# Gate and up products of the feed-forward layers in seven block products instead of eight

## Chip, core and metric

The kernel runs on one core of one Trainium2 chip. The metric is the device time of one execution in microseconds (us). The engines are TensorE (PE, with its weight loads as PEld), VectorE (DVE), ScalarE (ACT), GpSimd (POOL) and SyncE (SP, which here issues most of the loads).

## What is computed

One inference step of a small decoder trunk, all in float32, for 512 prompt tokens and 8 sample tokens (520 columns). There are two layers; each has a feed-forward block before and after its mixer, so four feed-forward layers run:

```
def _swiglu(h, wg, wu, wd):
    return (jax.nn.silu(h @ wg) * (h @ wu)) @ wd

for i in range(DEPTH):                      # DEPTH = 2
    x = x + 0.5 * _swiglu(_rmsnorm(x, norm_ffn1[i]), ffn1_wg[i], ffn1_wu[i], ffn1_wd[i])
    # mixer: chunked gMLP (i = 0) or S5 state-space scan (i = 1)
    x = x + out
    x = x + _cross_attn(_rmsnorm(x, norm_x[i]), mem_k[i], mem_v[i], x_wq[i], x_wo[i])
    x = x + 0.5 * _swiglu(_rmsnorm(x, norm_ffn2[i]), ffn2_wg[i], ffn2_wu[i], ffn2_wd[i])
```

The model width is 1024 (8 k-tiles of 128), the hidden width is 2816 (22 tiles of 128).

## The kernel before

Activations are kept transposed: `X` holds 8 tiles of 128 features x 520 tokens. Each product runs in three matmuls: every operand is split into a high part (rounded to the fast float32 matmul format) and a low remainder, and high x high, high x low and low x high are added up in PSUM. `wsplit` (L110, L113) makes the two parts of 128 columns of weights: ACT writes `wh`, then DVE, or POOL for every fourth, subtracts to get `wl`. `split` (L139, L140) does the same for activations. `lin` issues the matmuls; all go through `mm`, so line L74 stands for nearly all of them. A matmul covers 260 tokens, half of the 520; an accumulator `ps` holds both halves, and there are four of them.

A feed-forward layer (`ffn`) takes x times the norm's gain as eight tiles `xs`; the scale per token, `rs`, is applied later. It then walks over 11 blocks of 256 columns. `gu(j)` loads 256 columns of gate and 256 of up (SP queue, three buffers `wr`), splits them (four buffers each of `wh` and `wl`), and for each 128 of them runs 48 matmuls for gate and 48 for up. DVE multiplies both by `rs` (L345, L347), ACT takes silu (L346), DVE multiplies (L348), and `split` writes a tile of `hid`. After every six tiles of `hid` (`FFN_GROUPS`) `down` multiplies them by the down weights and DVE adds the results to `X` (L361). One more block is always done ahead of a `down`. In the last layer of all, `last` takes the final group and `finish` interleaves the output.

`fill()` is called after each block and each `down` and traces a step of side work: memory keys and values and the gMLP's matrices during the first layer, and the S5 mixer's tables (`s5_prep`, mostly POOL, with DVE, ACT and PE pieces) during the second and third. The last layer has none. Temporary tiles `t` come from 12 buffers, large tiles (`xs`, `hid`, the tables) from 22 slots.

The order of instructions on each engine is fixed before the run by a scheduler that takes what is ready by its own cost figures, in priority of the program's order; at run time each engine follows that order and waits by semaphore.

Of the kernel before, what the change touches and what calls it, by code (L numbers as in the profile page):

```python
# [9 lines left out]
F32 = mybir.dt.float32  # L10
# [22 lines left out]
SLOTS = 22  # L33
WB = 4
FFN_GROUPS = ((0, 6), (6, 12), (12, 18), (18, 22))
BUFS = {"t": 12, "rs": 2, "rt": 4, "st": 10, "sti": 4, "mv": 4, "sc": 2, "cj": 2, "s5": 12, "s5i": 1,
# [3 lines left out]
class Prog:  # L40
# [15 lines left out]
    # ---------------------------------------------------------------- helpers  # L56
# [16 lines left out]
    def mm(self, out, lhsT, rhs, start, stop):  # L73
        self.nc.tensor.matmul(out, lhsT=lhsT, rhs=rhs, start=start, stop=stop)  # L74
# [5 lines left out]
    def in_order(self, *engines):  # L80
        """The engines issue what is traced here in the order of the program."""
# [21 lines left out]
    def wsplit(self, raw, m, eng=None):  # L103
        """128 columns of weights as two parts."""
# [11 lines left out]
    def wload(self, src, nk, cols):  # L116
        """A block of weights [(nk 128), cols], split into two parts per 128 columns."""
        raw = self.wraw(nk, cols)
        self.wget(raw, src, 0, cols)
        return [self.wsplit(raw, m) for m in range(cols // 128)]  # L120

    def lin(self, ps, w, xs, k0=0, k1=None, hs=(0, 1)):
        """ps[:, :, :HN] = w^T @ xs; only the k-tiles k0 to k1 and the halves hs of the tokens."""
# [93 lines left out]
    def rsqrt(self, out, var, scale):  # L217
        """out = (var * scale + eps) ** -0.5 for a few columns: a first guess and Newton steps."""
# [16 lines left out]
    def rs_tok(self, sq):  # L235
        """rsqrt(mean_d x[t]^2 + eps) per token, tokens on partitions: four chunks and the last 128 tokens."""
# [8 lines left out]
    def rs_diag(self, sq):  # L245
        """The same on the diagonals of squares, for rs_row."""
# [8 lines left out]
    def rs_row(self, dg):  # L255
        """The scales along the free dimension, the same in every partition."""
# [7 lines left out]
    def scaled(self, key, xs, n0=0, n1=NT):  # L264
        """x * gain in two parts per k-tile."""
# [6 lines left out]
    def norm(self, key):  # L272
        """x * gain in two parts per k-tile; the scale per token comes later."""
# [4 lines left out]
    # -------------------------------------------------------------------- ffn  # L278
    def ffn(self, l, pre, fill=lambda: None, start=False, finish=None):
# [12 lines left out]
        def begin():  # L292
            """The first columns, the first half of the tokens before the second has come."""
# [59 lines left out]

        def down(a, b):
# [10 lines left out]
        def last(a, b):  # L365
            """The last columns, one half of the tokens after the other, each followed by its part of finish."""
# [27 lines left out]
        for g0, g1 in FFN_GROUPS:  # L394
            while done < min(DFF // 256, g1 // 2 + 1):
                gu(done)
# [6 lines left out]
    # ----------------------------------------------------------- memory k, v  # L403
    def mem_kv(self, l, kvd):
        """Steps that put the memory's keys (transposed) and values into DRAM, kvd."""
# [68 lines left out]
    # -------------------------------------------------------- cross-attention  # L474
    def attn(self, l, kvd):
# [28 lines left out]
        # sample queries as rows, spread over all partitions one batch entry at a time  # L504
# [75 lines left out]
        # one column of 32 per batch entry, so that every (b, h) adds up in its own row  # L580
# [39 lines left out]
        def part(k0, k1):  # L620
            """Heads of the first 256 columns of the output, for the first half of the tokens."""
# [55 lines left out]
    # ---------------------------------------------------------- chunked gMLP  # L677
    def gmlp_prep(self, mixw):
        """Steps that make the causal mixing weights, transposed; their row sums; the bias per row."""
# [22 lines left out]
    def gmlp(self, mixw):  # L702
# [6 lines left out]
        # v: gelu, then tokens on the partitions; [token, (j, chunk, column)] per pair of column tiles  # L709
# [71 lines left out]
        # the sample rows, one token per chunk: mixed = w_s[0, 0] * v + b_s[0]  # L781
# [73 lines left out]
    # -------------------------------------------------------------------- S5  # L855
    def dexp(self, x, sh, em1=None):
        """exp(x), and exp(x) - 1 when asked for."""
# [21 lines left out]
    def s5_prep(self):  # L879
        """Steps that make the matrices and tables of the scan and put them in DRAM."""  # L880
# [34 lines left out]
        # theta in turns: wh (few bits) + wl  # L915
# [71 lines left out]
        # C and B-bar with the state on the partitions  # L987
# [3 lines left out]
        for c, n in enumerate("re im".split()):  # L991
            nc.gpsimd.dma_start(cr[c], ins["b_c_" + n][0].rearrange("(t g) c p -> (g c) t p", t=8))
            nc.gpsimd.dma_start(bn[:, c], ins["b_b_" + n][0].rearrange("(q g) p c -> (g p) q c", g=2))
# [130 lines left out]
    def s5(self, fill=lambda: None):  # L1124
# [11 lines left out]
        def lay(i):  # L1136
            """[8 sample | 128 blocks | 8 sample] columns per place in the block."""
# [10 lines left out]
        def spread(u4):  # L1148
            """Places in the block onto the partitions, per pair of groups."""
# [27 lines left out]
        def scan(i, sps):  # L1177
            """The states of the four pairs of groups of channel tile i."""
# [91 lines left out]
        def states():  # L1270
            """New states of the samples and last states of the prompt."""
# [29 lines left out]
    # ------------------------------------------------------------------ final  # L1301
    def final(self):
        """What follows the columns q of the last product for the tokens of half h."""
# [137 lines left out]
```

## Time and profile before

| | us |
|---|---|
| median of three runs | 2496.0 |
| lowest run | 2494.11 |
| highest run (stands far from the others) | 8334.05 |
| span of the profiled execution | 2493.1 |

The median lies 2.9 us above the profiled span and the lowest run 1.0 us; no time of its own is recorded for the profiled execution beside its span. PE has 20575 matmuls and as many weight loads. Busy times overlap across engines. A granted clock of 1.00 is the full TensorE clock.

### The profile page before, as it was taken

To read this page: it belongs to the slowest core of one execution; us is meant where nothing else is said; L and a number is where in the kernel's file an instruction comes from. 1 tells how busy PE (TensorE), PEld (TensorE's weight loads), DVE (VectorE), ACT (ScalarE), POOL (GpSimd) and SP (SyncE) were. 2 spreads that over 40 slices of the span, in tenths; PEclk is the share of its full clock that TensorE was granted. 3 is DMA by queue.
4 is the path that set the end of the run, shared out by engine and by line. 5 is a ranking of instruction groups with operands and counts; after the bars stand their busy time and mean duration, and the time that the engine had idled before them with its cause. 6 is when DMAs were issued, how large, how long until landed. Compare 5 with 4: busy or idle time off the path is not lost.

```text
span 2493.1 us, 47609 instructions
## 1 busy us (share of the span) xinstructions
PE 2419.0 (97%) x20575; PEld 2364.9 (95%) x20575; DVE 1342.0 (54%) x2304; ACT 803.6 (32%) x1239; POOL 556.4 (22%) x532
## 2 busy tenths in 40 slices
PE   8999999999999999999999999999779999999998
PEld 7999999999999799999999999999769969999998
DVE  6534343648556557455565645536973655434344
ACT  4323232432224342232342422424322324222223
POOL 2111011102111012262523515103452101101111
PEclk8999999999999999999999999999889999999999
DMA  5243432321225623334233324327523562232321
GB/s 171 94 131 114 136 102 85 119 85 55 85 90 198 226 96 90 102 100 138 98 111 110 131 95 132 122 69 247 192 87 107 169 237 85 80 107 83 96 77 52
DMA packets 247376, 293.40 MB, mean 118 GB/s; under 512 B 7358, under 2 KB 226230, under 8 KB 247166
## 3 DMA queue, kind: packets, MB, share of 16 engines
q1 hardware_dynamic: 234055, 254.88, 31.5%
q10 hardware_dynamic: 12567, 34.38, 3.9%
q8 instruction: 162, 2.65, 0.4%
q0 software_dynamic: 544, 1.10, 0.3%
q14 instruction: 48, 0.39, 0.0%
HBM read 264.77 MB, written 25.56 MB: 116 GB/s over the span
## 4 chain that ended last, share of the span: by engine, by line
PE 88%; DVE 6%; issue 2%; ACT 2%; POOL 1%; DMA 1%; DVEq 0%; ACTq 0%; POOLq 0%
PE ps L74 86%; PE ps L77 2%; DVE ld L1194 1%; DVE v L773 1%; DVE xs L269 1%; DVE sq L213 1%; DVE wl L113 0%; DVE t L533 0%; POOL ld L1190 0%; DMA vc<-in_cache_mem_v 0%; DVE hid L140 0%; ACT e L553 0%; ACT wh L110 0%; DMA ld<-s5tt 0%; DVE bi L1093 0%
## 5 line engine op out<-in xcount | busy, mean ns | idle before, releaser
L74 PE MATMUL ps<-xs,wh 128*128 128x260 f32 x7168 | 1164.1, 284 | 3.4 <-ACT xs L268 2.4
L74 PEld LDWEIGHTS ps<-xs,wh 128*128 128x128 f32 x7168 | 990.0, 189 | 6.8 <-ACT xs L268 2.8
L110 ACT ACTIVATE wh<-wr 128x1024 fp32r<-128x1024 f32 (+2 forms) x440 | 420.3, 958 | 1161.1 <-PE ps L74 1051.4
L74 PE MATMUL ps<-xs,wl 128*128 128x260 f32 x3584 | 725.9, 283 | 0.0
L113 POOL TENSOR_TENSOR wl<-wr,wh 128x1024 fp32r<-128x1024 f32 (+2 forms) x119 | 271.4, 2281 | 1608.0 <-ACT wh L110 1580.3
L74 PEld LDWEIGHTS ps<-xs,wl 128*128 128x128 f32 x3584 | 554.4, 189 | 0.0
L74 PE MATMUL ps<-hid,wh 128*128 128x260 f32 (+2 forms) x2816 | 457.0, 283 | 2.7 <-ACT hid L139 1.8
L113 DVE TENSOR_TENSOR wl<-wr,wh 128x1024 fp32r<-128x1024 f32 (+2 forms) x321 | 365.9, 1140 | 98.5 <-ACT wh L110 97.0
L74 PEld LDWEIGHTS ps<-hid,wh 128*128 128x128 f32 x2816 | 388.5, 188 | 4.6 <-ACT hid L139 2.4
L74 PE MATMUL ps<-hid,wl 128*128 128x260 f32 (+2 forms) x1408 | 288.0, 282 | 0.0
L74 PEld LDWEIGHTS ps<-hid,wl 128*128 128x128 f32 x1408 | 218.9, 188 | 0.0
L347 DVE TENSOR_TENSOR t<-ps,rs 128x520 f32<-128x520 f32 x88 | 61.4, 698 | 254.5 <-PE ps L74 254.5
L361 DVE SCALAR_TENSOR_TENSOR X<-ps,X 128x520 f32<-128x520 f32 x120 | 83.7, 698 | 211.6 <-PE ps L74 211.1
L345 DVE TENSOR_TENSOR t<-ps,rs 128x520 f32<-128x520 f32 x88 | 61.4, 697 | 182.5 <-PE ps L74 151.6
L140 DVE TENSOR_TENSOR hid<-t,hid 128x520 fp32r<-128x520 f32 x88 | 95.5, 1086 | 34.3 <-ACT hid L139 34.3
L139 ACT ACTIVATE hid<-t 128x520 fp32r<-128x520 f32 x88 | 56.3, 639 | 127.5 <-DVE t L348 127.4
L74 PE MATMUL ps<-o,wh 128*128 128x260 f32 x512 | 92.5, 290 | 1.2 <-DVE o L140 0.7
L74 PE MATMUL ps<-ms,wh 128*128 128x256 f32 x512 | 92.0, 282 | 0.8 <-DVE ld L1187 0.5
L74 PE MATMUL ps<-z,wh 128*128 128x260 f32 x512 | 84.6, 286 | 1.1 <-DVE z L140 0.5
L348 DVE TENSOR_TENSOR t<-t,t 128x520 f32<-128x520 f32 x88 | 78.9, 896 | 6.8 <-ACT wh L110 0.5
L74 PE MATMUL ps<-um,wh 128*128 128x260 f32 x512 | 82.5, 283 | 0.0
L74 PEld LDWEIGHTS ps<-o,wh 128*128 128x128 f32 x512 | 74.6, 188 | 7.4 <-issue 2.9
(316 smaller groups left out, 2406.3 us busy)
## 6 DMA issues: line engine op xcount, KB each, us to landing
wr<-in_ffn_wg SPq DMA_DIRECT2D x43, 1024.0 KB, 5.3
wr<-in_ffn_wu SPq DMA_DIRECT2D x43, 1024.0 KB, 5.2
wr<-in_ffn_wd SPq DMA_DIRECT2D x48, 768.0 KB, 4.8
wr<-in_a_w_in SPq DMA_DIRECT2D x16, 1024.0 KB, 5.8
kc<-in_cache_mem_k SPq DMA_DIRECT2D x32, 512.0 KB, 7.7
vc<-in_cache_mem_v SPq DMA_DIRECT2D x32, 512.0 KB, 5.8
wr<-in_x_wk SPq DMA_DIRECT2D x8, 1024.0 KB, 5.2
wr<-in_x_wv SPq DMA_DIRECT2D x8, 1024.0 KB, 5.2
```

What stands on the lines that cost most here:

```text
L74: self.nc.tensor.matmul(out, lhsT=lhsT, rhs=rhs, start=start, stop=stop)
L77: self.nc.tensor.transpose(out, in_, self.ident[base : base + k, base : base + k])
L110: nc.scalar.activation(hi, r, AF.Copy)
L113: eng.tensor_sub(lo, r, hi.bitcast(F32))
L139: nc.scalar.activation(sl[:, 0, n0:n1], src, AF.Copy)
L140: nc.vector.tensor_sub(sl[:, 1, n0:n1], src, sl.bitcast(F32)[:, 0, n0:n1])
L213: (nc.gpsimd if k == 7 and early or k < 4 and not early else nc.vector).tensor_add(sums[-1], sums[-1], t)
L269: self.nc.vector.scalar_tensor_tensor(s[:, 1, n0:n1], x, g, s.bitcast(F32)[:, 0, n0:n1], op0=ALU.mult, op1=ALU.subtract)
L345: nc.vector.tensor_mul(self.v2(t), pg[:, :, :HN], rs)
L347: nc.vector.tensor_mul(self.v2(w), pu[:, :, :HN], rs)
L348: nc.vector.tensor_mul(w, w, t)
L361: nc.vector.scalar_tensor_tensor(xv, p[:, :, :HN], 0.5, xv, op0=ALU.mult, op1=ALU.add)
```

## The change

All blocks of gate and up but the first of each layer go through `gu7` instead of `gu`. Weights and tokens are cut into 2 x 2 blocks: the 256 columns of a block into two halves of 128, the 1024 features into two halves of 512, the tokens into two halves of 260. The eight block products become seven, each of 24 matmuls for gate and up together; their operands are sums and differences of blocks (`seven_x` for the tokens, once per layer; `seven` for the weights, per block), and the results are sums of products, partly added in PSUM (an accumulator is written on after DVE has read it), partly by DVE. All low parts of these weights are DVE's. The down products take groups of four hidden tiles instead of six (the last layer of all ends as before), there are two more slots, two fewer temporary tiles, and one S5 transfer is cut into parts so that a smaller scratch suffices. The diff, without lines that only drop comments:

```diff
-SLOTS = 22
+SLOTS = 24
-FFN_GROUPS = ((0, 6), (6, 12), (12, 18), (18, 22))
-BUFS = {"t": 12, ...
+FFN_GROUPS = ((0, 4), (4, 8), (8, 12), (12, 16), (16, 20), (20, 22))
+END_GROUPS = ((0, 4), (4, 8), (8, 12), (12, 18), (18, 22))
+BUFS = {"t": 10, ...
+    def seven_x(self, key, xs):
+        xb = [[self.slot([128, 4, HN], F32, "xb") for _ in range(2)] for _ in range(2)]
+        for k in range(KT):
+            for h in range(2):
+                nc.scalar.activation(xb[k // 4][h][:, k % 4], self.X[:, k, h * HN : (h + 1) * HN], AF.Copy,
+                                     scale=self.gcol(key, k))
+        (b11, b12), (b21, b22) = xb
+        V.tensor_sub(b11, b12, b11)
+        V.tensor_sub(b12, b22, b12)
+        V.tensor_sub(b22, b22, b11)
+        V.tensor_sub(b21, b21, b22)
+        T = []
+        for b in (b11, b22, b12):
+            hi, lo = (self.slot([128, 4, HN], F32R, "xt") for _ in range(2))
+            nc.scalar.activation(hi, b, AF.Copy)
+            V.tensor_sub(lo, b, hi.bitcast(F32))
+            T.append([(hi[:, k], lo[:, k]) for k in range(4)])
...
+        def last():
+            for k in range(4):
+                self.split(xs[k], b21[:, k], HN, NT)
+        return {"B11": B[0], "B21": B[2], "B22": B[3], "T1": T[0], "T2": T[1], "T3": T[2], "T4": B[1]}, last
+    def seven(self, r1, r2, ops, ps):
+        sh = list(r1.shape[:3]) + [128]
+        A11, A21, A12, A22 = r1[..., :128], r1[..., 128:], r2[..., :128], r2[..., 128:]
+        n, nk = sh[1:3]
+        def parts(src):
+            hi = self.wp.tile(sh, F32R, name=self.nm("wh"), tag="wh", bufs=WB)
+            lo = self.wp.tile(sh, F32R, name=self.nm("wl"), tag="wl", bufs=WB)
+            nc.scalar.activation(hi, src, AF.Copy)
+            V.tensor_sub(lo, src, hi.bitcast(F32))
+            return hi, lo
+        def product(p, w, b, first):
+            hi, lo = w
+            for x in range(n):
+                for k in range(nk):
+                    bh, bl = ops[b][k]
+                    for i, (m, r) in enumerate(((hi, bh), (hi, bl), (lo, bh))):
+                        self.mm(p[:, x, :HN], m[:, x, k], r, first and k == 0 and i == 0, k == nk - 1 and i == 2,
+                                skip_group_check=not first)
+        S1, S2 = (self.wp.tile(sh, F32, name=self.nm("S"), tag="S", bufs=2) for _ in range(2))
+        w11 = parts(A11)
+        G.tensor_add(S1, A21, A22)
+        G.tensor_sub(S2, S1, A11)
+        a, b, c = (ps() for _ in range(3))
+        va, vb, vc = (p[:, :, :HN] for p in (a, b, c))
+        e1, e2, e3 = (self.tmp([128, 2, HN]) for _ in range(3))
+        product(a, w11, "B11", True)
+        nc.scalar.copy(e1, va)
+        product(b, parts(S2), "T2", True)
+        V.tensor_add(e2, vb, e1)
+        product(a, parts(A12), "B21", False)
+        yield "11", va
+        V.tensor_sub(A21, A11, A21)
+        V.tensor_sub(A12, A12, S2)
+        product(b, parts(A21), "T3", False)
+        V.tensor_add(e3, vb, e1)
+        product(c, parts(S1), "T1", True)
+        V.tensor_add(e3, vc, e3)
+        yield "22", e3
+        product(b, parts(A22), "T4", False)
+        V.tensor_add(e1, vb, e1)
+        yield "21", e1
+        product(c, parts(A12), "B22", False)
+        V.tensor_add(e2, vc, e2)
+        yield "12", e2
+        def gu7(j):
+            if ops is None:
+                ops, late = self.seven_x(key, xs)
+                late()
...
+            for i in range(2):
+                r.append(self.wp.tile([128, 2, 4, 256], F32, name=self.nm("wr"), tag="wr", bufs=3))
+                for x, w in enumerate((wg, wu)):
+                    nc.sync.dma_start(r[i][:, x], w[i * 512 : (i + 1) * 512, cs].rearrange("(k p) m -> p k m", p=128))
+            tw = [self.tmp() for _ in range(2)]
+            for name, v in self.seven(*r, ops, self.ps):
+                i, h = int(name[0]) - 1, int(name[1]) - 1
+                d = self.tmp([128, 2, HN]) if name == "11" else v
+                nc.vector.tensor_mul(d, v, rs[:, h : h + 1].to_broadcast([128, 2, HN]))
+                nc.scalar.activation(d[:, 0], d[:, 0], AF.Silu)
+                nc.vector.tensor_mul(tw[i][:, h * HN : (h + 1) * HN], d[:, 1], d[:, 0])
+                if name in ("21", "12"):
+                    hid[2 * j + i] = self.slot(name="hid")
+                    self.split(hid[2 * j + i], tw[i])
+            fill()
-        for g0, g1 in FFN_GROUPS:
+        for g0, g1 in END_GROUPS if finish else FFN_GROUPS:
-                gu(done)
+                (gu7 if done else gu)(done)
-            nc.gpsimd.dma_start(bn[:, c], ins["b_b_" + n][0].rearrange("(q g) p c -> (g p) q c", g=2))
+            for q in range(0, NPAIR, 16):
+                nc.gpsimd.dma_start(bn[:, c, q : q + 16], ...
-    nc = bacc.Bacc("TRN2", target_bir_lowering=False, num_devices=1)
+    nc = bacc.Bacc("TRN2", target_bir_lowering=False, num_devices=1, dynamic_dma_scratch_size=4096)
```

## Rows read from the trace of the kernel before

**Rows 1.** The page, parts 1 and 4: busy shares; the chain that ended last.

```profile
...
PE 2419.0 (97%) x20575; PEld 2364.9 (95%) x20575; DVE 1342.0 (54%) x2304; ACT 803.6 (32%) x1239; POOL 556.4 (22%) x532
...
PE 88%; DVE 6%; issue 2%; ACT 2%; POOL 1%; DMA 1%; DVEq 0%; ACTq 0%; POOLq 0%
PE ps L74 86%; PE ps L77 2%; DVE ld L1194 1%; DVE v L773 1%; DVE xs L269 1%; DVE sq L213 1%; DVE wl L113 0%; DVE t L533 0%; POOL ld L1190 0%; DMA vc<-in_cache_mem_v 0%; DVE hid L140 0%; ACT e L553 0%; ACT wh L110 0%; DMA ld<-s5tt 0%; DVE bi L1093 0%
...
```

**Rows 2.** Windows: layers, first block, two blocks, a down product, a burst.

```profile
core 0: us, PE busy (x) PEld busy (x) DVE busy (x) ACT busy (x) POOL busy (x), PEclk, DMA share, GB/s
...
32.00:440.00 408.00, 407.25 (x3367) 405.62 (x3368) 174.07 (x220) 122.60 (x161) 50.50 (x22) 0.99 0.35 112
910.00:1297.00 387.00, 383.28 (x3223) 381.02 (x3222) 217.32 (x375) 122.16 (x186) 130.47 (x160) 1.00 0.32 101
1297.00:1690.00 393.00, 388.13 (x3281) 384.78 (x3280) 215.54 (x332) 130.89 (x203) 125.02 (x154) 1.00 0.35 115
2094.00:2470.00 376.00, 376.00 (x3136) 375.56 (x3135) 164.36 (x204) 103.57 (x132) 44.27 (x23) 1.00 0.26 82
2094.00:2117.00 23.00, 23.00 (x192) 22.88 (x191) 14.24 (x29) 9.09 (x11) 2.42 (x1) 1.00 0.29 92
2131.00:2177.00 46.00, 46.00 (x387) 46.00 (x386) 20.76 (x23) 13.14 (x17) 5.61 (x2) 1.00 0.24 75
2192.00:2227.00 35.00, 35.00 (x294) 35.00 (x293) 12.65 (x15) 7.85 (x9) 4.24 (x2) 1.00 0.37 121
...
1065.00:1090.00 25.00, 25.00 (x212) 25.00 (x211) 12.79 (x12) 6.09 (x9) 19.67 (x37) 1.00 0.13 37
```

**Rows 3.** The chain in order of time: start us, us, what.

```profile
...
480.01 5.75 PE ps L74 x48
...
2139.99 328.32 PE ps L74 x2738
...
2476.68 2.85 PE ps L74 x24
...
```

**Rows 4.** Groups by shape: busy us, mean ns of one, idle before, releaser.

```profile
...
L110 ACT ACTIVATE wh<-wr 128x1024 fp32r<-128x1024 f32 x288 | 304.5, 1059 | 835.5 <-PE ps L74 735.0 <-issue 75.3 <-DVE t L1114 21.6
...
L361 DVE SCALAR_TENSOR_TENSOR X<-ps,X 128x520 f32<-128x520 f32 x120 | 83.7, 698 | 211.6 <-PE ps L74 211.1
...
L345 DVE TENSOR_TENSOR t<-ps,rs 128x520 f32<-128x520 f32 x88 | 61.4, 697 | 182.5 <-PE ps L74 151.6 <-POOL M L1041 30.5
...
L139 ACT ACTIVATE hid<-t 128x520 fp32r<-128x520 f32 x88 | 56.3, 639 | 127.5 <-DVE t L348 127.4
...
L268 ACT ACTIVATE xs<-X,gains 128x260 fp32r<-128x260 f32 x16 | 6.7, 500 | 0.0
...
```

**Rows 5.** DVE in order of time, last layer: start us, us, operation.

```profile
...
2155.34 1.22 DVE L113 TENSOR_TENSOR wl<-wr,wh 128x1024 fp32r<-128x1024 f32 x1
2156.48 0.69 DVE L140 TENSOR_TENSOR hid<-t,hid 128x520 fp32r<-128x520 f32 x1
...
2167.62 2.11 DVE L140 TENSOR_TENSOR hid<-t,hid 128x520 fp32r<-128x520 f32 x1 [0.70 <-ACT hid L139]
...
2192.86 0.69 DVE L361 SCALAR_TENSOR_TENSOR X<-ps,X 128x520 f32<-128x520 f32 x1
2193.47 0.95 DVE L113 TENSOR_TENSOR wl<-wr,wh 128x768 fp32r<-128x768 f32 x1
...
```

**Rows 6.** POOL in order of time, the same stretch.

```profile
...
2166.36 2.81 POOL L113 TENSOR_TENSOR wl<-wr,wh 128x1024 fp32r<-128x1024 f32 x1 [20.18 <-ACT wh L110]
...
2223.86 2.39 POOL L113 TENSOR_TENSOR wl<-wr,wh 128x1024 fp32r<-128x1024 f32 x1 [15.62 <-ACT wh L110]
...
```

**Rows 7.** DVE in order of time, a layer that prepares S5.

```profile
...
1081.94 3.49 DVE L113 TENSOR_TENSOR wl<-wr,wh 128x1024 fp32r<-128x1024 f32 x1
...
```

**Rows 8.** Waits: us in total, times, longest us.

```profile
...
DVE t L345 <- POOL M L1041: 30.5, 4, 7.6
...
```

**Rows 9.** DMA issues: KB each, median us from issue to landing.

```profile
...
wr<-in_ffn_wg SPq DMA_DIRECT2D x43, 1024.0 KB, 5.3
...
```

More of the change, by code (lines that the diff above doesn't have):

```diff
@@ L32 @@
 MAGIC = 12582912.0
-SLOTS = 22
+SLOTS = 24
 WB = 4
-FFN_GROUPS = ((0, 6), (6, 12), (12, 18), (18, 22))
-BUFS = {"t": 12, "rs": 2, "rt": 4, "st": 10, "sti": 4, "mv": 4, "sc": 2, "cj": 2, "s5": 12, "s5i": 1,
+FFN_GROUPS = ((0, 4), (4, 8), (8, 12), (12, 16), (16, 20), (20, 22))
+END_GROUPS = ((0, 4), (4, 8), (8, 12), (12, 18), (18, 22))
+BUFS = {"t": 10, "rs": 2, "rt": 4, "st": 10, "sti": 4, "mv": 4, "sc": 2, "cj": 2, "s5": 12, "s5i": 1,
         "s5r": 2}
@@ L71, in const, with mm @@
         return self.cp.tile(list(shape), dt, name=name, tag=name)
-    def mm(self, out, lhsT, rhs, start, stop):
-        self.nc.tensor.matmul(out, lhsT=lhsT, rhs=rhs, start=start, stop=stop)
+    def mm(self, out, lhsT, rhs, start, stop, **kw):
+        self.nc.tensor.matmul(out, lhsT=lhsT, rhs=rhs, start=start, stop=stop, **kw)
     def tr(self, out, in_, k=128, base=0):
@@ L276, in norm @@
         return xs, self.squares()
+    def seven_x(self, key, xs):
+        nc = self.nc
+        V = nc.vector
+        xb = [[self.slot([128, 4, HN], F32, "xb") for _ in range(2)] for _ in range(2)]
[14 more added lines that the diff above has]
+            T.append([(hi[:, k], lo[:, k]) for k in range(4)])
+        B = [[(xs[4 * i + k][:, 0, h * HN : (h + 1) * HN], xs[4 * i + k][:, 1, h * HN : (h + 1) * HN])
+              for k in range(4)] for i, h in ((0, 0), (0, 1), (1, 0), (1, 1))]
+        def last():
+            for k in range(4):
+                self.split(xs[k], b21[:, k], HN, NT)
+        return {"B11": B[0], "B21": B[2], "B22": B[3], "T1": T[0], "T2": T[1], "T3": T[2], "T4": B[1]}, last
@@ new lines, in seven @@
+    def seven(self, r1, r2, ops, ps):
+        nc = self.nc
+        V, G = nc.vector, nc.gpsimd
+        sh = list(r1.shape[:3]) + [128]
[41 more added lines that the diff above has]
+        yield "12", e2
@@ L352, in gu @@
             fill()
+        ops = None
+        def gu7(j):
+            nonlocal ops
+            if ops is None:
+                ops, late = self.seven_x(key, xs)
+                late()
+            cs = slice(j * 256, (j + 1) * 256)
+            r = []
+            for i in range(2):
[13 more added lines that the diff above has]
+            fill()
         def down(a, b):
@@ L992, in s5_prep @@
             nc.gpsimd.dma_start(cr[c], ins["b_c_" + n][0].rearrange("(t g) c p -> (g c) t p", t=8))
-            nc.gpsimd.dma_start(bn[:, c], ins["b_b_" + n][0].rearrange("(q g) p c -> (g p) q c", g=2))
+            for q in range(0, NPAIR, 16):
+                nc.gpsimd.dma_start(bn[:, c, q : q + 16],
+                                    ins["b_b_" + n][0, 2 * q : 2 * q + 32].rearrange("(q g) p c -> (g p) q c", g=2))
         yield
```

## The prediction

> **What bounds the kernel now.** I read the page first. TensorE (PE) is busy for 97% of the span, and 88% of the chain that ended last is PE, nearly all of it on the one matmul line L74 [rows 1]. So the span is close to a plain count of matmuls, and what removes matmuls removes time unless something else comes late. The second view is the table of windows [rows 2]: in each of the four feed-forward layers PE is busy for 99 to 100% of the stretch at a granted clock of 0.99 to 1.00 (2.4 GHz). The engines beside it differ by layer. VectorE (DVE) works 44% of the last layer; in the two layers that also prepare the S5 mixer DVE works 55 to 56% and GpSimd (POOL) 32 to 34%, against POOL's 12% in the others. Two gate-and-up blocks alone take 46.0 us, with 20.8 us of DVE, 13.1 of ScalarE (ACT) and 5.6 of POOL.
>
> The third view is the chain [rows 3]. It gives the price of a matmul of 260 columns: 5.75 us for 48, 328.32 us for 2738, so 119.8 to 119.9 ns. The weight order of the new products (three matmuls in a row into the same accumulator half, each with its own weight load) is that of today's last product, where 24 take 2.85 us, 119 ns. I price old and new alike.
>
> **What goes.** A block of 256 gate and 256 up columns has 192 matmuls today, 23.0 us; seven products of 24 make 168, 20.1 us, 2.9 us each. The first block of a layer stays, so ten blocks in four layers change: 40 x 24 = 960 matmuls, x 119.8 ns = 115 us. That is all the change can bring. The down products keep their count.
>
> **What comes, on each engine.** DVE per new block, spaced as back-to-back starts in the trace [rows 5]: 1.14 us for 1024 columns from SBUF, 0.61 for 520. Seven low parts 8.0; the two in-place weight differences 2.3; five sums of products 3.0; four scalings by rs 2.4; four half-width gate times up, about 0.35 each (estimate, half of 0.61 plus a little), 1.4; two low parts of hid 1.2. Sum 18.4 of 20.1 us, against 10.4 now [rows 2]. ACT: 7 x 1.06, 4 silu halves and 3 wider copies, 10.9 us [rows 4]; not a bound. POOL: two sums of 1024 columns, 2.39 us each when undisturbed [rows 6], 4.8 against 2.8 now.
>
> None of this is on PE's path as long as it runs ahead. Today each split waits for PE to free a buffer [rows 4], so four products are in hand, and four will still be. The read-outs of accumulators are tighter: product 4 overwrites what DVE must have read after product 2, product 6 what it read after 4, and 7 what it read after 5. Each has one product, 2.9 us, less 0.70 for the read [rows 4] and a few tenths for signals: 1.9 us of patience in DVE's queue, three times a block. The copy after product 1 is ACT's, 0.64 us; it hides.
>
> **(a) Sums of the tokens.** They are made once a layer beside the first block. ACT: 16 x 0.50 [rows 4], three high parts at 1.06 and four short ones, 13 us. DVE: 7 x 1.14 + 4 x 0.35 = 9.4. That block's window now has ACT busy 9.1 and DVE 14.2 of 23.0 us [rows 2], so both would be full, and the second product needs its operand 2.9 us after the window. I take 2 us a layer, 8 in all; between 0 and the whole 9.4 of DVE (38 in all).
>
> **(b) GpSimd's sums against VectorE.** While POOL runs a two-input operation from 2166.36 to 2169.17, DVE's 0.70 us subtraction takes 2.11 [rows 5, 6], 1.4 us lost; another split, 1.22 undisturbed [rows 5], takes 3.49 in a layer with POOL's preparation [rows 7], 2.3 lost. Reads of accumulators aren't hit (L345 has a mean of 697 ns over 88 instructions, L361 698 over 120) [rows 4]. Now where do the sums fall? After each pair of blocks comes a down product, in which DVE works 12.7 of 35 us [rows 2]. The sums for a pair's first block run under it; those for the second run inside the first. There DVE has 20.1 - 18.4 = 1.7 us free, and 2.2 more, since no preceding block leaves its last read-out behind: 3.9. At the whole 2.39 twice, 4.8, it is over by 0.9. I take 1 us for each of the 20 pairs, 20 us, from the dearer row, since a DVE at 92% seldom has a gap to meet POOL in. Between 0 (the mean loss of 1.4 twice, 2.8, fits) and 20 x 4.8 = 96, if no free time can be used.
>
> The Trainium skill, page "SBUF — State Buffer", section "SBUF: two separate sides", says that a DVE operation with two SBUF inputs and a GpSimd operation reading SBUF exclude each other for the whole instruction. That speaks against this change, which adds both kinds. The row of 2.11 us agrees in kind but shows only 1.4 us lost. By the page's whole hold (b) is 20 and the time 2432; by the 1.4 us of that row (b) is 0 and the time 2412.
>
> **(c) Helper tiles in the two S5-preparing layers.** A block takes six helper tiles "t" of ten; today it takes four of twelve. Already today read-outs wait for a tile that POOL's preparation holds, four times, up to 7.6 us and 30.5 us together [rows 8], and PE lost nothing because another accumulator was free. With the read-outs tight, (7.6 - 1.9) x 4 = 23 us reach PE. Between 0 and the whole gain of the two layers, 57. The slots go with this: the token sums keep six, so 14 of 24 are taken before hid, where 8 of 22 were; that can hold back the preparation, which drains at the end of the second of these layers, and I put it inside these bounds.
>
> **Answered at nothing.** X read-outs: six groups for four (five in the last layer) are 56 more at 0.70 us, 39 us of DVE under down products, where it is idle for 64%; 39 if that cover were gone. Loads: same bytes in four transfers a block. The second weight tile is asked for when the fourth split ends (about 2.6 us into a block), lands 5.3 us later [rows 9], sums 4.8, split 2.3: 15.4 us, needed at 23.0; DVE's lateness must pass 7.6 us before this counts, and then the sums and the weight loads behind them on SP's queue are late together. The cut of the B matrices' transfer and the smaller scratch: nothing.
>
> **The sum.** 2493.1 - 115 + 8 + 20 + 23 = 2429. The lowest run of before and the median lie 1.0 and 2.9 us above the profiled span; against the median I add 2.9: 2432 us, 2.6% faster. Two per cent, about 50 us, is what a measurement of this kernel can tell from no change, so under 2446 is faster and over 2546 slower.
>
> **Rivals.**
> 1. Everything hides: a, b and c are 0, 2493 - 115 + 3 = 2381. For it: the down products give DVE some 12 us of slack after each pair, and POOL's burst of 19.7 busy us in 25 cost PE nothing today (1065 to 1090) [rows 2]. Against it: three read-outs a block with 1.9 us of patience.
> 2. The two S5 layers gain nothing. POOL works 130 and 125 us there today and DVE 217 and 216 [rows 2]; DVE gains some 8 us a block, 80, and POOL 20. That is 297 + 150 = 447 us of work for two engines that mostly exclude each other, in a layer of 358 to 364; only about 75 us of it reads accumulators and may overlap. So (c) is 57 and the other layers' (a) and (b) 14: 2493 - 115 + 57 + 14 + 3 = 2452. Against it: the preparation's POOL work can slide into down products.
> 3. Slower: the three read-outs wait behind a POOL hold each time. A read-out that queues behind a held split waits 2.39 + 1.22 and takes 0.70, 4.3 us where 2.9 are allowed: 1.4 lost, x 120 = 168 us, with (a) and (c) 31: 2493 - 115 + 168 + 31 + 3 = 2580. It decides from 0.7 us a read-out (84 / 120). Against it: there are two POOL sums a block, not three, and in half of the blocks they run under a down product.
>
> **How the numbers follow.** The forecast (2400 to 2450) gets 0.38, rival 1 0.17, rival 2 0.35 (spread 2440 to 2505), rival 3 0.10. The range 2380 to 2505 takes in the first three, and leaves out rival 3 and the tails, under 0.2. Faster: 0.34 of the forecast, 0.17, 0.04 of rival 2, 0.55. Same: 0.04, 0.31 and 0.01 of rival 3, 0.36. Slower 0.09.
>
> **What the profile will show.** PE has 960 instructions fewer, 19615, else the change isn't what it says. Window of a block pair: 40.2 us if all hides, 41 for (b), and over 45 for rival 3. DVE busy near 1342 + 400 = 1750 us or more with the holds, POOL near 650. In the waits, PE behind DVE's sums of products in the S5 layers shows (c), and PE behind the token sums after the first block (a). The prediction is wrong if the order on DVE puts splits ahead of read-outs everywhere, since then PE waits in every block, or if late loads show on SP's queue.

## The result and the profile after

The changed kernel takes 2646.7 us in the median (2644.1 to 2652.8, four runs) against 2495.2 for the kernel before on the same chip: 1.061 times as long, 95% interval 1.060 to 1.063. I had forecast 2432, and the range ended at 2505. The sign was wrong.

The page of the changed kernel, parts 1, 2 and 4 (answers to [rows 1]):

```profile
span 2645.1 us, 47424 instructions
...
PE 2392.1 (90%) x19615; PEld 2322.4 (88%) x19615; DVE 1860.2 (70%) x2966; ACT 1005.8 (38%) x1627; POOL 712.6 (27%) x588
...
PEclk8999999999999989989898989999989999999999
...
PE 11%; DVE 3%; issue 2%; DMA 1%; POOL 1%; ACT 0%; SPq 0%; DVEq 0%; POOLq 0%; ACTq 0%
```

The matmuls went as counted: 20575 - 19615 = 960. The chain, 88% PE before [rows 1], now covers only 18% of the span by its own shares, so I read it no further. Two subtractions on part 1 give the account. PE stood idle for 2493.1 - 2419.0 = 74 us before and for 2645.1 - 2392.1 = 253 now, 179 more. And PE's busy time should have fallen by 115 to 2304, but is 2392, 88 more, for matmuls of the same size. 179 + 88 = 267, which is the 152 us of the result and the 115 that should have gone.

Most of the 88 is the clock. The mean granted clock over the span fell from 0.988 to 0.948; with the two levels of 0.50 (1.2 GHz) and 1.00 (2.4 GHz) that is (1 - 0.948) x 2 x 2645 = 275 us at the low level against 60 before. TensorE was busy in 198 us of that and in 45 before; at full clock the 153 more would have taken half, so some 77 of the 88 are the clock's, and the other 11 stay open. Windows of the changed kernel (columns as in [rows 2]): the first layer, the two that prepare S5 (as two equal halves of their stretch), the last, and then three stretches around one stop of PE:

```profile
12.00:467.00 455.00, 423.26 (x3396) 419.84 (x3395) 337.11 (x426) 195.57 (x298) 101.25 (x44) 0.95 0.36 112
931.00:1387.00 456.00, 385.15 (x2976) 375.16 (x2976) 339.07 (x549) 168.20 (x274) 190.51 (x222) 0.91 0.27 87
1387.00:1843.00 456.00, 400.33 (x3149) 392.68 (x3148) 353.21 (x501) 192.54 (x321) 151.92 (x126) 0.93 0.33 107
2230.00:2630.00 400.00, 371.70 (x2955) 368.60 (x2954) 293.21 (x371) 155.87 (x229) 74.21 (x36) 0.95 0.25 79
2354.00:2357.20 3.20, 0.05 (x2) 0.05 (x1) 3.20 (x4) 1.83 (x2) 1.00 (x1) 0.86 0.01 2
2357.20:2363.20 6.00, 6.00 (x28) 6.00 (x29) 4.20 (x6) 1.03 (x2) 0.00 (x0) 0.50 0.27 86
2363.20:2380.00 16.80, 16.80 (x142) 16.80 (x142) 14.29 (x19) 7.91 (x12) 0.00 (x0) 1.00 0.20 64
```

A stop of 3.2 us is followed by 6.0 us at 0.50, in which 28 matmuls run, 214 ns each; in the stretch behind it 142 take 16.8 us, 118 each. At 118 ns the 28 would have taken 3.3 us, so this stop of 3.2 us costs about 6.

In the table, a layer runs from the start of its first matmul to that of its last; "priced" takes 28.7 us for 240 matmuls off each layer of before.

| us | first | two S5 layers | last | the rest |
|---|---|---|---|---|
| before | 448.0 | 792.1 | 385.0 | 868.0 |
| priced | 419.3 | 734.6 | 356.3 | 868.0 |
| after | 456.3 | 912.0 | 402.2 | 874.6 |
| lost | 37.0 | 177.4 | 45.9 | 6.6 |

The last layer has no side work, so it shows the block by itself. VectorE, GpSimd and TensorE in order of time before the stop above; three views of the changed kernel (start us, us, operation, idle before it and what ended it):

```profile
2346.41 1.23 DVE L329 TENSOR_TENSOR wl<-wr,wh 128x1024 fp32r<-128x1024 f32 x1 [0.20 <-ACT wh L328]
2351.54 1.23 DVE L355 TENSOR_TENSOR wr<-wr 128x1024 f32<-128x1024 f32 x1 [3.90 <-POOL S L344]
2352.68 0.69 DVE L463 TENSOR_TENSOR t<-ps,rs 128x520 f32<-128x520 f32 x1
2353.29 2.80 DVE L329 TENSOR_TENSOR wl<-wr,wh 128x1024 fp32r<-128x1024 f32 x1
2356.01 0.42 DVE L465 TENSOR_TENSOR t<-t 128x260 f32<-128x260 f32 x1
2356.35 0.69 DVE L358 TENSOR_TENSOR t<-ps,t 128x520 f32<-128x520 f32 x1
```

```profile
2349.12 2.38 POOL L344 TENSOR_TENSOR S<-wr,wr 128x1024 f32<-128x1024 f32 x1 [13.35 <-DMA wr<-in_ffn_wu]
2351.58 3.42 POOL L345 TENSOR_TENSOR S<-S,wr 128x1024 f32<-128x1024 f32 x1
```

```profile
2357.18 0.77 PE L75 MATMUL ps<-xs,wh 128*128 128x260 f32 x2 [3.15 <-DVE t L358]
```

L358 is the read-out after product 4 that product 6 must await. L355 is the first in-place difference of the *next* block. DVE's order has it ahead of L358, and it waits 3.90 us for GpSimd's first sum (L344), which waited for the second weight tile to land. Then the low part L329 takes 2.80 us where the one at 2346.41 took 1.23: GpSimd's second sum (L345) runs beside it. Two causes stand in one stop, so the experiments had to part them: a wait in the wrong place, and operations made longer by GpSimd's reads.

The waits of the changed kernel (us in total, times, longest us):

```profile
POOL S L344 <- DMA wr<-in_ffn_wu: 306.5, 27, 35.5
...
DVE wr L355 <- POOL S L344: 131.8, 32, 15.2
...
PE ps L75 <- ACT t L350: 54.0, 10, 15.3
...
PE ps L75 <- DVE t L358: 38.9, 11, 6.0
```

The third row is another place, the copy after product 1 (L350). ScalarE before the 7.25 us stop in the second block of the last layer, and TensorE at its end:

```profile
2264.19 6.53 ACT L293 ACTIVATE xb<-X,gains 128x260 f32<-128x260 f32 x16
2270.63 1.05 ACT L303 ACTIVATE xt<-xb 128x1040 fp32r<-128x1040 f32 x1
2271.59 0.56 ACT L350 COPY t<-ps 128x520 f32<-128x520 f32 x1
```

```profile
2272.20 0.80 PE L75 MATMUL ps<-xs,wh 128*128 128x260 f32 x2 [7.25 <-ACT t L350]
```

The 16 copies of the token sums and a high part stand ahead of a copy of 0.56 us. In the S5 layers the same copy also waits for a helper tile that GpSimd's preparation holds, and GpSimd's own splits stand behind its preparation (TensorE waited 7.9 us for one of them). The copy in such a layer:

```profile
1267.56 0.59 ACT L350 COPY t<-ps 128x520 f32<-128x520 f32 x1 [11.90 <-POOL M L1164]
```

### The profile page after: what moved, and what is told of

Its sections match the earlier page's. It is cut to its first block, busy times and chain, and to the rows that moved or that the text cites. A ratio compares the mean times of both kernels' runs of the same rounds, so it can differ in the third digit from the quotient of the medians.

```text
span 2645.1 us, 47424 instructions
## 1 busy us (share of the span) xinstructions
PE 2392.1 (90%) x19615; PEld 2322.4 (88%) x19615; DVE 1860.2 (70%) x2966; ACT 1005.8 (38%) x1627; POOL 712.6 (27%) x588
## 5 line engine op out<-in xcount | busy, mean ns | idle before, releaser
L75 PE MATMUL ps<-xs,wh 128*128 128x260 f32 x4608 | 860.3, 297 | 103.5 <-ACT t L350 54.0
L75 PEld LDWEIGHTS ps<-xs,wh 128*128 128x128 f32 x4608 | 722.8, 200 | 114.8 <-ACT t L350 56.4
L111 ACT ACTIVATE wh<-wr 128x512 fp32r<-128x512 f32 (+3 forms) x336 | 261.7, 782 | 543.8 <-PE ps L75 458.5
L75 PE MATMUL ps<-xt,wh 128*128 128x260 f32 x1920 | 360.0, 288 | 29.8 <-ACT xt L303 13.4
L75 PEld LDWEIGHTS ps<-xt,wh 128*128 128x128 f32 x1920 | 303.3, 193 | 33.6 <-ACT xt L303 14.4
L328 ACT ACTIVATE wh<-wr 128x1024 fp32r<-128x1024 f32 x200 | 210.8, 1057 | 245.6 <-PE ps L75 214.0
L329 DVE TENSOR_TENSOR wl<-wr,wh 128x1024 fp32r<-128x1024 f32 x200 | 288.4, 1443 | 11.7 <-ACT wh L328 10.9
L75 PE MATMUL ps<-xt,wl 128*128 128x260 f32 x960 | 273.4, 287 | 8.7 <-DVE wl L329 8.7
L114 DVE TENSOR_TENSOR wl<-wr,wh 128x512 fp32r<-128x512 f32 (+3 forms) x243 | 224.6, 925 | 48.6 <-ACT wh L111 47.9
L344 POOL TENSOR_TENSOR S<-wr,wr 128x1024 f32<-128x1024 f32 x40 | 98.9, 2472 | 392.8 <-DMA wr<-in_ffn_wu 306.5
L75 PEld LDWEIGHTS ps<-xt,wl 128*128 128x128 f32 x960 | 183.6, 192 | 9.2 <-DVE wl L329 9.1
L355 DVE TENSOR_TENSOR wr<-wr 128x1024 f32<-128x1024 f32 x40 | 62.0, 1551 | 131.8 <-POOL S L344 131.8
L345 POOL TENSOR_TENSOR S<-S,wr 128x1024 f32<-128x1024 f32 x40 | 136.3, 3408 | 33.6 <-DVE wl L329 31.0
```

Of the source, the lines that this page charges most:

```text
L111: nc.scalar.activation(hi, r, AF.Copy)
L114: eng.tensor_sub(lo, r, hi.bitcast(F32))
L328: nc.scalar.activation(hi, src, AF.Copy)
L329: V.tensor_sub(lo, src, hi.bitcast(F32))
L344: G.tensor_add(S1, A21, A22)
L345: G.tensor_sub(S2, S1, A11)
```

## The experiments

Medians are of four runs unless said. Each ratio is against the kernel before on the same chip, and "from" numbers are those of the changed kernel (2646.7). The stage times are read as in the table above, from one profiled run of each version; the last layer took 396.5 us instead of 402.2 in run 4, whose edit is not in that layer, so a layer's difference of some 6 us is not read as an effect by itself.

**1. Eight products in the new frame.** Which part belongs to the seven products at all?

```diff
-                (gu7 if done else gu)(done)
+                gu(done)
```

> All blocks by the old eight-product code; groups of four hidden tiles, 24 slots, 10 helper tiles, the cut S5 transfer and the small scratch stay. If the loss comes with the seven products: 2490 to 2510. If the frame around them (fewer helper tiles, POOL issuing four S5 transfers instead of two) costs by itself: 2530 or more, the excess in the second and third feed-forward layers.

2524.9 us, ratio 1.010 (1.008 to 1.013), between the two expectations. The layers take 446.5, 809.6 and 385.3, the rest 882.4. So smaller down groups, two helper tiles fewer, the cut transfer and the smaller scratch cost some 28 us, 17.5 of them in the S5 layers and 14 outside (where the changed kernel, with the same frame, shows only 6.6 more). I had put that at nothing. The seven products account for the other 122, on top of the 115 that they take off.

**2. The order on DVE.** The next block's two differences (L355, L356) come after this block's read-out L360, by an edge of the scheduler alone:

```diff
+        with self.tc.issue_after(self.read.ins) if self.read else nullcontext():
             V.tensor_sub(A21, A11, A21)
             V.tensor_sub(A12, A12, S2)
...
+        self.read = read            # the second read-out into e3, set at the end of the block
```

> One order edge: the in-place weight differences of a block go behind the previous block's third read-out on DVE's queue; same work. Queue-order theory (a DVE queue head that waits for POOL's sum and through it for the second weight tile blocks the read-out): the four waits of 3.4 to 4.5 us between products 5 and 6 in the last layer fall under 1 us each, its half-clock time falls from 37 to about 15 us, the last layer goes from 402 to about 380 us, the whole to 2590 to 2615. Hold theory (VectorE blocked while GpSimd reads): the waits stay over 1.5 us, the whole over 2625.

2606.1 us, ratio 1.044 (1.042 to 1.046): 40 us come back. The last layer takes 384.8 from 402.2. In the whole run TensorE waits for the read-out only in passing (10.9 us over nine times, the longest 1.8), and the last layer's time at the low clock falls from 37.5 to 17.1 us. The wait in the wrong place was real, but most of the loss stays.

**3. Token sums traced ahead of the first block** (not in the first layer, whose first block is written out by hand):

```diff
         done = 0
+        if not start:
+            ops, late = self.seven_x(key, xs)
```

> The sums of token blocks are traced ahead of the layer's first block in three layers (not the first). If ACT's queue is what stops PE at the second block (16 copies of 0.4 us ahead of the read-out of the first product): the waits of 7.5 to 8.1 us there go in three layers, with the half clock behind them 10 to 14 us a layer, the whole 2605 to 2620. If the sums only start PE's layer later instead: 2635 to 2660.

2633.5 us, ratio 1.055 (1.052 to 1.057), 13 us less, just outside the second expectation. The 7.25 us stop in the second block of the last layer is gone and that layer takes 395.7 from 402.2, but a stop of 4.6 us appears in its first block, ahead of the matmuls that spread the scale per token, and the S5 and attention stage before it takes 396.0 from 386.7.

**4. The S5 preparation taken out of its two layers** (it is run in the open, with a part of the second memory's keys, behind the second of them); a single run.

```diff
-        self.ffn(0, False, steps(prep))
+        self.ffn(0, False)
...
-        self.ffn(1, True, steps(pre))
+        self.ffn(1, True)
```

> The S5 preparation and the second memory's keys are traced behind the feed-forward layers instead of between their blocks. If POOL's preparation is what costs the second and third layers more than the last: those two take 800 to 820 us together, twice the last layer, instead of 912, and the whole may rise or fall with the preparation then left in the open (up to 150 us). If VectorE's load by the products alone is enough: they stay near 900.

2732.1 us as a whole, with the preparation now uncovered. The two layers take 788.2, with 237 matmuls moved out with it, 28 us: 816 on equal terms, from 912. So some 95 of their 177 us of loss need this side work, and the other 82 come without it, about twice the 45.9 of the last layer.

**5. Product 6 into a fourth accumulator**, so that it doesn't overwrite what L358 must read:

```diff
-        product(b, parts(A22), "T4", False)
-        V.tensor_add(e1, vb, e1)
-        yield "21", e1
+        f = ps()
+        product(f, parts(A22), "T4", True)
+        V.tensor_add(e4, f[:, :, :HN], e4)     # e4 holds the sum after product 4
+        yield "21", e4
```

> One edit: the sixth product of each block goes into a fourth accumulator, so that it no longer overwrites what VectorE must read after the fourth product; that read-out may be late by one product more. Queue theory (the waits between product 5 and 6 come from a read-out that stands behind a weight difference of the next block): the 3.4 to 4.5 us stops between products 5 and 6 go in all layers, the last layer takes about 382 us instead of 402, the first about 450, and the whole comes to 2600 to 2615 us, as with the order edge alone. Rival, VectorE is simply too full (holds by GpSimd's sums): the lateness is only passed on to product 7 and to the next block's first products, the last layer stays at 397 us or more and the whole at 2635 or more.

2621.7 us, ratio 1.051 (1.049 to 1.052), between the two expectations; the last layer takes 390.7. Product 6 no longer waits, but product 7 does: in the list of waits TensorE now stands 22.3 us, 11 times, for the next read-out (L360). Giving the read-out more room passes on part of DVE's lateness.

**6. Matmuls in the stop.** After product 5 of every second block in the first and last layer 24 more write columns that nobody reads:

```diff
         product(c, parts(S1), "T1", True)
+        for i in range(fillers):
+            self.mm(a[:, 0, HN:512], s1[0][:, 0, i % 4], ops["T1"][i % 4][0][:, :252], True, True, ...)
```

> One edit: behind the fifth product of every second block of the first and the last layer (four blocks in each) 24 more matmuls of 252 columns write columns that nobody reads, 24 x 4 x 2 = 192 matmuls, about 22 us of TensorE at full speed, where TensorE stops for 3.4 to 4.5 us now. Clock theory (a short stop costs more than its length because the granted clock is 0.5 for some us behind it): the stop is filled, half-clock time in the last layer falls from 37 us to under 20, and the added 2.8 us a time cost nothing or less: the last layer 390 to 402 us, the whole 2630 to 2648. Rival, the clock would have fallen anyway and the stops cost their length alone: the last layer grows by up to what isn't covered, 402 to 413 us, half-clock time stays, and the whole is at 2647 to 2665.

2644.1 us, ratio 1.060 (1.058 to 1.062): 192 more matmuls, 22.5 us of TensorE, for no change in time. In the last layer the time at 0.50 fell from 37.5 to 23.9 us, not under 20, and the layer took 399.6. So the low clock belongs to the stops: where one is filled there is less of it. The unchanged time alone couldn't show that, because a stop that ends with VectorE's read-out hides what fills it; and nothing is repaired.

**7. The sums on VectorE instead of GpSimd.**

```diff
-        G.tensor_add(S1, A21, A22)
-        G.tensor_sub(S2, S1, A11)
+        V.tensor_add(S1, A21, A22)
+        V.tensor_sub(S2, S1, A11)
```

> One edit: the two sums of weight quarters of each block are made by VectorE instead of GpSimd: 40 blocks x 2 x 1.15 us = about 46 of 40 x 2 ... 92 us more on VectorE, 100 us or more less on GpSimd, and no GpSimd read of weights while VectorE splits. Hold theory (GpSimd's sums cost VectorE more time than the sums are long, 2.5 to 3.4 us each against 1.15 for making them itself): the weight splits' mean falls from 1443 ns to about 1200, and the time falls, 2600 to 2635 us, most in the first and last layers, which have no other work of GpSimd's. Rival, VectorE's load and the order of its queue decide: the sums wait on VectorE for the second weight tile with everything behind them, the stops grow, and the time is the same or more, 2645 to 2720 us.

2546.0 us, ratio 1.021 (1.019 to 1.023): 100.7 us less, and lower than either expectation. The layers take 438.4, 854.9 and 369.8. The page, part 1, and the groups of two operations, of this run:

```profile
PE 2352.2 (92%) x19615; PEld 2287.8 (90%) x19615; DVE 1868.0 (73%) x3046; ACT 1008.1 (40%) x1627; POOL 479.1 (19%) x508
```

```profile
L329 DVE TENSOR_TENSOR wl<-wr,wh 128x1024 fp32r<-128x1024 f32 x200 | 246.5, 1235 | 10.3 <-ACT wh L328 9.6
...
L345 DVE TENSOR_TENSOR S<-S,wr 128x1024 f32<-128x1024 f32 x40 | 54.5, 1362 | 0.6
L344 DVE TENSOR_TENSOR S<-wr,wr 128x1024 f32<-128x1024 f32 x40 | 54.2, 1354 | 35.6 <-DMA wr<-in_ffn_wu 33.7 <-issue 1.8
```

and the same operations in the changed kernel:

```profile
L329 DVE TENSOR_TENSOR wl<-wr,wh 128x1024 fp32r<-128x1024 f32 x200 | 288.4, 1443 | 11.7 <-ACT wh L328 10.9
```

```profile
L345 POOL TENSOR_TENSOR S<-S,wr 128x1024 f32<-128x1024 f32 x40 | 136.3, 3408 | 33.6 <-DVE wl L329 31.0
...
L344 POOL TENSOR_TENSOR S<-wr,wr 128x1024 f32<-128x1024 f32 x40 | 98.9, 2472 | 392.8 <-DMA wr<-in_ffn_wu 306.5 <-ACT xb L293 35.9 <-ACT wh L328 21.9
```

VectorE took on 108.7 us of sums and its busy time grew by 7.8. So the other 101 us had been in its old operations; added up one by one these fell by 90, since neighbours overlap by up to 0.1 us and the busy time counts that once. While GpSimd summed for 235 us (136.3 + 98.9), VectorE's old work was some 90 to 101 longer. In the last layer a block pair now takes 40.2 us of TensorE's time, where the changed kernel took 46.4 and 46.2. The sums are also made faster, 1.35 us each instead of 2.5 and 3.4.

**8. Twelve helper tiles, 23 slots** (from 10 and 24).

```diff
-SLOTS = 24
+SLOTS = 23
-BUFS = {"t": 10, ...
+BUFS = {"t": 12, ...
```

> One edit: twelve helper tiles instead of ten, and 23 slots instead of 24, so that the S5 preparation holds fewer of those that a block's copies and sums of products wait for. Tile theory (step (c) as predicted): the two waits of ScalarE's copy for a tile that GpSimd's preparation holds (24 us in all, TensorE stopped for some 14 us at each, with the low clock behind) go, and the middle two layers take 870 to 890 us instead of 912, the whole 2605 to 2625. Rival, the preparation's own work on VectorE and GpSimd decides: the tiles only let it run further ahead, the middle layers stay at 900 to 915 us and the whole at 2635 to 2650.

2633.3 us, ratio 1.056 (1.054 to 1.057), 13 less and short of both expectations: the S5 layers take 897.7 from 912.0. The two waits of L350 for the preparation are still there, 19.4 us from 23.8. More tiles let the preparation run ahead and take them too.

**9. GpSimd busy again, with nobody waiting for it.** Run 7 removed both the longer operations and the wait of L355 for GpSimd. This run has the sums on VectorE, and GpSimd makes differences of the same weights for no reader:

```diff
+        for half in range(2):
+            H = self.wp.tile([sh[0], 1, nk, 128], F32, name=self.nm("H"), tag="H", bufs=1)
+            for _ in range(2):
+                G.tensor_sub(H, A22[:, half : half + 1], A11[:, half : half + 1])
```

> The sums of weight quarters are made by VectorE, as in the run with that one edit (2546.0 us; last layer 369.8 us), and GpSimd beside it makes as many differences of the same weights (2048 columns a block, in four pieces) into a tile that nobody reads. So GpSimd's work is back and no engine waits for it. (23 slots and 11 helper tiles make room for that tile.) Hold theory, now in the form that what GpSimd's sums cost is the time that VectorE's own two-input operations lose beside them: the weight splits' mean goes from 1235 ns back to 1380 or more, the last layer takes 385 us or more, and the whole 2580 to 2640. Rival, the wait is what cost (VectorE stood 131.8 us at the in-place difference for GpSimd's result, and reads of accumulators behind it): the splits may lengthen, but the last layer stays at 369 to 378 us and the whole at 2545 to 2565.

2667.0 us, ratio 1.070 (1.068 to 1.071): 121 more than run 7 and above the 2640 that I had expected at most, and the last layer back at 401.5. The page, part 1, and a group of GpSimd's:

```profile
PE 2394.6 (90%) x19615; PEld 2321.8 (87%) x19615; DVE 1991.9 (75%) x3046; ACT 1007.9 (38%) x1627; POOL 793.9 (30%) x668
```

```profile
L349 POOL TENSOR_TENSOR H<-wr,wr 128x512 f32<-128x512 f32 x160 | 291.1, 1820 | 434.0 <-DMA wr<-in_ffn_wg 388.5 <-issue 35.4 <-DMA wr<-in_ffn_wu 1.8
```

VectorE's busy time is 123.9 us longer than in run 7, for the same 3046 instructions. VectorE and GpSimd in order of time, in the last layer:

```profile
2447.08 1.23 DVE L344 TENSOR_TENSOR S<-wr,wr 128x1024 f32<-128x1024 f32 x1 [2.65 <-DMA wr<-in_ffn_wu]
2448.22 0.69 DVE L467 TENSOR_TENSOR t<-ps,rs 128x520 f32<-128x520 f32 x1
2448.83 1.71 DVE L329 TENSOR_TENSOR wl<-wr,wh 128x1024 fp32r<-128x1024 f32 x1
2450.47 1.49 DVE L469 TENSOR_TENSOR t<-t 128x260 f32<-128x260 f32 x1
2451.88 2.28 DVE L345 TENSOR_TENSOR S<-S,wr 128x1024 f32<-128x1024 f32 x1
2454.09 0.69 DVE L362 TENSOR_TENSOR t<-ps,t 128x520 f32<-128x520 f32 x1
2454.69 1.21 DVE L329 TENSOR_TENSOR wl<-wr,wh 128x1024 fp32r<-128x1024 f32 x1
```

```profile
2445.75 7.33 POOL L349 TENSOR_TENSOR H<-wr,wr 128x512 f32<-128x512 f32 x4 [10.77 <-DMA wr<-in_ffn_wg]
```

GpSimd works from 2445.75 to 2453.08. In that time VectorE's two-input operations on SBUF take 1.71, 1.49 and 2.28 (L344 alone keeps its 1.23: it ran while GpSimd's second piece, begun with it, took 2.33 against 1.30 for the first); behind it the low part is back at 1.21. The operations that read an accumulator (L467, L362) keep their 0.69. The low parts' mean came to 1336 ns, less than the 1380 I had expected: the sums, which lie nearest to GpSimd's work, took the larger share. The run isn't a pure copy of the changed kernel: GpSimd's extra work is 291 us instead of 235, and VectorE has the sums on top. In the stretch shown VectorE also stood 2.65 us for the second weight tile, over the run 39.5 us against 33.7 in run 7, so the last layer's stops aren't the longer operations' alone; why that tile came later there isn't shown. What the run shows is that GpSimd's reads bring the loss back with no engine waiting for their result.

**10. The order edge on top of run 7** (both diffs).

> The sums on VectorE and the order edge together (the next block's in-place weight differences after this block's last early read-out). Order alone took 40 us off with the sums on GpSimd. If the order matters only because the differences wait for GpSimd's result, the edge has nothing left to mend: 2535 to 2556 us, no change that can be told from 2546. Rival, the order is a cost of its own (two differences of 1.25 us and what is behind them ahead of the read-out, whoever makes the sums): 2505 to 2530.

2547.6 us, ratio 1.021 (1.018 to 1.023), no change from run 7. The order mattered only because the differences waited for GpSimd; its 40 us are part of the 100.7, not beside them.

**11. All that helped, seven products in all layers**: runs 3, 7 and 8 together, and the S5 matrices' transfers issued by ScalarE (`nc.scalar.dma_start` for `nc.gpsimd.dma_start`).

> Seven products in all layers with four edits together: sums on VectorE (2546 alone), token sums ahead of the first block, twelve helper tiles and 23 slots, the S5 matrices' transfers issued by ScalarE. The last two cost theories that single edits gave 13 us each, and TensorE's wait of 8 us behind the transfers on GpSimd. If they add up: 2508 to 2528 us. Rival, with the sums on VectorE the other waits are hidden or only exchanged for each other: 2535 to 2550.

2509.3 us, ratio 1.006 (1.005 to 1.008). The last layer takes 359.7, 3.4 from its price; the S5 layers 828.4, still 94 over theirs and 36 over before.

**12. Seven products only in the first and last layer**: runs 3, 7 and 8, token sums ahead in the last layer, and the S5 layers with eight products and the old groups.

```diff
+MID_GROUPS = ((0, 6), (6, 12), (12, 18), (18, 22))
-                (gu7 if done else gu)(done)
+                (gu7 if done and (start or finish) else gu)(done)
```

> Seven products only in the first and the last layer, with the sums on VectorE, token sums made ahead of the first block in the last layer, twelve helper tiles and 23 slots; the two middle layers, which prepare the S5 mixer, as in the kernel before. From the stages measured: first layer about 438 (448 before), last about 363 to 370 (385 before), the middle two 792 to 802 (792 before), the mixers up to 8 each more than before. Sum: 2468 to 2495 us, the first version that is no slower than the kernel before. Rival, the frame (slots, tiles, smaller transfers) costs the middle layers and mixers as much as in the run with eight products (28 us): 2495 to 2510.

2465.1 us, ratio 0.989 (0.987 to 0.991), 28 us or 1.1% under the kernel before and the only version here that beats it. Its page, part 1, and its windows of the last layer and the two S5 layers:

```profile
PE 2367.3 (96%) x20095; PEld 2311.1 (94%) x20095; DVE 1608.2 (65%) x2668; ACT 904.5 (37%) x1429; POOL 510.6 (21%) x520
```

```profile
2092.60:2451.20 358.60, 357.27 (x2974) 356.05 (x2973) 293.83 (x390) 157.95 (x232) 21.38 (x19) 1.00 0.27 89
915.70:1707.70 792.00, 783.38 (x6601) 777.80 (x6601) 439.13 (x713) 259.96 (x398) 264.11 (x321) 1.00 0.34 113
```

The last layer takes 358.6 us, 26.4 of the 28.7 that seven products were to bring, at a granted clock of 1.00 and with VectorE at 82%, as much VectorE time as in the changed kernel. The S5 layers are at 792 as before: with the old groups and twelve helper tiles back, the frame's 17.5 us there are gone.

## Why the prediction was wrong, by its steps

**What goes.** Right to the instruction: 960 matmuls, and run 12 delivers their price where nothing stops TensorE.

**(b), the step that failed.** I priced GpSimd's sums against VectorE at 20 us, between 0 and 96. Moving them away is worth 100.7, and some 90 to 101 us of VectorE's time were lost beside them. The first is above my upper end, the second about at it. The working went wrong in its currency: it set the work of a block against VectorE's free time in that block (3.9 us free, 4.8 asked, "over by 0.9") and let every loss that fitted into free time cost nothing. But I had also written that a read-out has 1.9 us of patience, three times a block. One held operation of 2.80 us in the queue ahead of it uses that up, however idle VectorE is a few us later. That was rival 3; its price, 1.4 us a read-out, came from these same rows, and I gave it 0.10. Its sign came too: over 45 us for a block pair, and 46.4 and 46.2 in the last layer, against 40.2, the value for "all hides", once VectorE makes the sums (run 7). The sums were also mis-sized: 2.39 us each from [rows 6], but 2.47 and 3.41 in the changed kernel, since GpSimd is held as well.

My estimate of VectorE's work was good: "near 1342 + 400 = 1750 us or more with the holds" against 1868.0 - 108.7 = 1759 without sums or most holds, in run 7. What the engine had to do was not the trouble, but when.

The rule cited from the Trainium skill, page "SBUF — State Buffer", section "SBUF: two separate sides", named the resource: run 9 shows longer operations where both read SBUF, and accumulator reads that stay at 0.69. The Trainium skill's page "Perfetto Trace Analysis", section "Optimizing Scalar/DVE Operations", warns that offloading work between VectorE and GpSimd might not help, since they share a read port. For the sums on GpSimd the trace goes further: they cost 100.7 us against the same sums on VectorE (run 7).

**"Loads: nothing".** I gave the second weight tile a margin of 7.6 us until its sums are needed, by product 2 of the next block (the terms add up to 15.0 us and not 15.4, so 8.0). It ended much earlier: VectorE's order puts the next block's difference L355 ahead of a read-out of this block, so a late tile and GpSimd's sum of it become a wait of this block. Run 2 shows 40 us for it. The prediction's last paragraph named this danger only for splits, and as a condition, with no price. With the sums on VectorE the edge brings nothing more (run 10), though VectorE itself still stands 33.7 us for that tile.

**(a) Token sums.** Priced at 8 us, at most 38. The longest stops at the second blocks are 15.3, 7.4, 7.8 and 7.3 us, 38 in all, before the shorter ones beside them and the low clock behind them. I had added up how much work each engine gets and missed that ScalarE's part of it, 7.6 us in the last layer, stands in one piece ahead of a copy of 0.56 us. In the last layer making them early brings 10 to 11 us (runs 11 and 12 against run 7, with the helper tiles changed too); the first layer's stop, 14 to 19 us, stays in every version with seven products, and at 16.5 is most of the 19 us by which it misses its price in run 12.

**(c) The S5 layers.** The waits for helper tiles came, as two of 11.9 us on ScalarE's copy and not four on VectorE; TensorE's stops there are 7.2 and 6.9, so 14 us before the clock where I had priced 23. The layers lost 177 us, beyond the whole gain of 57 that I had made the bound. A step that removes work can also cost more than that work. Rival 2 had the overload of VectorE and GpSimd right and stopped at "gain nothing". By run 4, 95 of the 177 need the preparation and the keys traced with it. Run 11 still loses 94 there, after all the mends; that these are the same 95 isn't shown, and which of the preparation's waits carries most of them stays open.

**The clock, which I didn't price.** 77 of the 267 us. All windows that I read before showed 0.99 to 1.00 [rows 2], and I took that as a property of the layer, when it belonged to a TensorE that never stopped. The sum of added stops has to be taken some 40% larger here, 77 on 179.

**The frame.** 28 us (run 1) where I had written nothing or put it inside (c). One part is a wait for an X read-out, which I had answered at nothing: 7.9 us of TensorE in run 1 and 9.2 in the changed kernel, and none as long with twelve helper tiles (run 8).

## What to carry to other kernels

Where a change makes TensorE wait for short read-outs, price it by what can stand ahead of each of them in its engine's fixed order, longest operation and longest wait included, not by the engine's free time in a block. Before giving GpSimd work that reads SBUF beside a VectorE that is busy with two-input operations, price it as VectorE's time too: here GpSimd's 235 us cost VectorE some 90 to 101, nearly the 109 that the work takes on VectorE itself. And where TensorE ran without a stop, add to every stop that the change brings the low clock behind it.

## What the runs showed of the hardware

- GpSimd and VectorE lengthen each other: GpSimd's second sum took 3.4 us in the mean against 2.39 in [rows 6]; VectorE's 1.22 us low parts took up to 2.8 in the last layer, which has no side work. The loss was about 0.4 us of VectorE for each us of GpSimd's work in both runs that show it (90 to 101 of 235, 124 of 291).
- VectorE's reads of an accumulator of 520 columns kept 0.69 us beside GpSimd's work; the longest of the changed kernel's 296 took 0.70.
- After a stop of 3.2 us TensorE ran for 6.0 us at a granted clock of 0.50, 214 ns a matmul instead of 118.
